# Moving seven pieces of side work, and splitting the mean term of a last layer norm into rows, in a two-block transformer kernel

## The chip, the cores and the metric

The kernel runs on one core of a Trainium2 chip. The metric is the device time of one execution in microseconds (us), the median of three runs. A profile is taken in an execution of its own, which has a time of its own.

## The reference

One sequence of 256 tokens and width 2048 goes through two blocks, all in fp32. The first block has four mixers side by side on one projection, an output projection, and a gated feed-forward. The second has an attention mixer and a retention mixer, each followed by a layer norm. Cut to the parts that the change touches:

```python
def first_block(x, ...):                       # T = 256, D = 2048
    h = rms_norm(x, norm_mix)
    a_q, a_kv, a_g, b_cols, c_cols, d_cols = jnp.split(h @ w_in, SPLIT_POINTS, axis=-1)
    o_a = nsa_attention(...)                   # heads with compressed, selected, window parts
    o_b = short_conv_mixer(b_cols, conv_w)     # 3-tap convolution times a gate
    o_c = spatial_gating_mixer(c_cols, sgu_w, sgu_b)   # gelu, layer norm, token mixing, gating
    o_d = stick_breaking_attention(dq, dk, dv)
    mixed = rms_norm(stack([o_a, o_b, o_c, o_d]), group_gain)
    x = x + mixed @ w_out
    h = rms_norm(x, norm_ffn)
    return x + (silu(h @ w_ffn_gate) * (h @ w_ffn_up)) @ w_ffn_down

def second_block(x, ...):
    y = attention_mixer(x, ...)                # q, k, v, gate; 16 heads; (o * silu(g)) @ w_out
    x = layer_norm(ALPHA * x + y, ln_gain[0], ln_bias[0])
    y = retention_mixer(x, ...)                # 8 heads forward and backward, group norm, gate
    return layer_norm(ALPHA * x + y, ln_gain[1], ln_bias[1])
```

## The kernel before

**Matrix products.** The weights come from HBM as units of up to 1024 columns by 128 rows (`wf`, fetched from SyncE's queue, four buffers). ScalarE rounds a unit into `wh` (L375) and VectorE forms the rest `wl = wf - wh` (L385), four buffers each. `job_T` multiplies a unit's 128x128 chunks with an activation tile that holds a high and a low part side by side: one matmul of 512 columns with `wh` (L452) and one of 256 with `wl` (L453), called a pair here. Four output tiles of 128 rows collect in four PSUM banks (`st`); at the end of a job an `evac` callback empties each bank. The last chunks of a job (`tail` of them) are run output by output, so that the four banks end one after the other instead of together. `job_N` is the same with the roles of weights and activations exchanged, three matmuls of 512 columns (L475 to L477). One matmul form with two extra columns (L441 to L443) serves the layer norm that is folded into the next projection.

**Side work.** Everything else (attention heads, gelus, norms, splitting of activations into high and low) is written as Python generators in a scheduler `S`. Each pair advances a counter, and every second pair is a tick; `yield n` puts the rest of a generator n ticks later. A generator only fixes where instructions are issued: each engine then runs its own in that order. When a matmul needs an activation tile that its generator has not made yet, `XS.__getitem__` forces the generator's remaining steps on the spot, in one burst. `S.drain` does the same.

**Stage a** is the projection `w_in` (jobs for the mixers A, D, C, B in turn) with the generators `task_A`, `task_D`, `task_C` and `by_task`/`task_B`; it ends with the job whose banks `ev_bb(2)` empties. `task_A` and `task_D` and `task_C` share two PSUM banks `mA`. `task_C` handles two halves of 128 tokens one after the other: gelu of `cv` (L702 to L710), a layer norm with `rsqrt` (a chain of ten tiny VectorE operations, L496 to L501), `v` scaled at L1043, gelu of `cu`, then the token mixing on PE (L1048), L1049 and L1051 on VectorE, and `finish_nat`: a square sum on ScalarE (L717), an `rsqrt`, transposes (L725) and the split into `xB` tiles (ScalarE L732, VectorE L738). **Stage b** is `w_out`: four jobs `wo(0)` to `wo(3)` that read the 16 tiles `xB` (0 to 3 from A, 4 to 7 from D, 8 to 11 from C, 12 to 15 from B) and whose banks VectorE empties (L1144, L1145). Inside `wo(0)` the tile `xB[8]` is wanted at pair 32 of 64, and a burst is forced there if `task_C` is not done.

**Bank emptying in `ev_bb`** (two output tiles, i = i0 and i0 + 1): ScalarE copies the right half (L662), VectorE adds the left (L664), then a product with `zy[i]` from `by_task(i)` (L1095), its square (L1100) and the sum `bacc` (L1101) run on GpSimd, and for the last tile (i = 3) on VectorE. `by_task` uses GpSimd at L1068, L1069 and L1077.

**Later.** The attention mixer of the second block makes its heads one after the other; `og_task` gates a head's output (L1522) and, ten ticks later, splits it (ScalarE L509, VectorE L511) for the output projection. In that projection, `stat(k)` adds each finished tile (L1432, L1434) to the sums of the next layer norm: a square on ScalarE (L1369), the sum on GpSimd (L1370), the sum of squares on GpSimd for k < 12 and on VectorE above (L1372). The column sums on PE (L1393) follow.

**The end.** The last layer norm needs mean and variance of full rows. After the last matmul, VectorE finishes the statistics and makes `nm = -mean * rstd` (L1990). For six of the eight 128x512 output pieces, the product of the gain with `nm` plus the bias is a K = 2 matmul in plain fp32 (L2004), from the rows `[nm, 1]` and `[gain, bias]`; L2011 adds it to the scaled row, and each piece is stored from the queue of SyncE or of ScalarE (L2012).

Of the kernel before, what the change touches and what calls it, by code (L numbers as in the profile page):

```python
# [9 lines left out]
F32 = mybir.dt.float32  # L10
F32R = mybir.dt.float32r
I32 = mybir.dt.int32
AF = mybir.ActivationFunctionType
OP = mybir.AluOpType
# [4 lines left out]
P = 128  # L19
T = 256  # L20
D = 2048
# [186 lines left out]
def pack_inputs(inp):  # L208

    f = {k: np.asarray(v) for k, v in inp.items()}  # L210
# [54 lines left out]
    qg, kg = f["attn_q_gain_2"][0], f["attn_k_gain_2"][0]  # L265
    out["v3"] = np.ascontiguousarray(rep(np.concatenate([qg, qg[sw], kg, kg[sw]])))
    c = shape_consts()
    out["lnv"] = np.ascontiguousarray(np.stack([f["ln_gain_2"][1], f["ln_bias_2"][1]]))
    out["ident"] = c["ident"]
    out["c1"] = np.concatenate([c[k] for k in C1], 1)  # L270
# [68 lines left out]
def body(tc, a, out, stop=None, dbg=None):  # L339
# [142 lines left out]
    def take():  # L482
        return jq.pop(0)
# [176 lines left out]
    def ev_sum(p, mk=s1):  # L660
        t = mk("evt")
        ACT.activation(t, p[:, T:], AF.Copy)  # L662
        s = mk("evs")
        V.tensor_tensor(s, p[:, :T], t, OP.add)  # L664
        return s
# [82 lines left out]
    def task_A():  # L748
# [36 lines left out]
        for tt in range(2):  # L785
# [25 lines left out]
                            gate[tt][:, 0:8].rearrange("p (g i) -> p i g", g=2), OP.mult)  # L811
            V.tensor_tensor(w, w, wt[:, :, None].to_broadcast([P, 8, nk]), OP.mult)
            V.tensor_tensor(w, w, cmk[:, None, 15 * tt:15 * tt + nk].to_broadcast([P, 8, nk]), OP.mult)
            yield 1
            pt = mA()
            PE.transpose(pt[:120, :P], sc, ident)
            pcT = small(128)
            V.tensor_copy(pcT[:120], pt[:120, :P])
            yield 1
            po = pm.tile([P, 512], F32, name="mO", tag="mO", bufs=1)  # L820
            PE.matmul(po, pcT[:120], vc[:120].rearrange("p c d -> p (c d)"), start=True, stop=True)
            per, nkt = (4, 1) if tt == 0 else (2, 2)
# [211 lines left out]
    def task_C():  # L1034
        yield tSg
        yield tD
        for tt in range(2):
            v = yield from gelu2(cv[tt], 512, s2)
            st_, mv, r = small(6), small(2), small()
            V.bn_stats(st_, v)  # L1040
            V.bn_aggr(mv, st_)
            rsqrt(r, mv[:, 1:2], 1.0, 4e-5, 1)
            V.tensor_scalar(v, v, mv[:, 0:1], r, OP.subtract, OP.mult)  # L1043
            u = yield from gelu2(cu[tt], 512, s2)
            yield 1
            pz = mA()
            for h in range(8):
                PE.matmul(pz[:, h * 64:h * 64 + 64], sg[h // 4][:, h % 4, :], v[:, h * 64:h * 64 + 64], start=True, stop=True)  # L1048
            V.tensor_tensor(v.rearrange("p (h e) -> p h e", h=8), pz.rearrange("p (h e) -> p h e", h=8),  # L1049
                            sgb[:, :, None].to_broadcast([P, 8, 64]), OP.add)  # L1050
            V.scalar_tensor_tensor(u, u, 0.5, v, OP.mult, OP.mult)  # L1051
            yield 3
            yield from finish_nat(u, 8, tt, mA)
# [33 lines left out]
    def ev_bb(i0):  # L1087
        def f(m, p):
            i = i0 + m
            s = ev_sum(p)  # L1090
            S.drain(tBy[i])
            last = i == 3
            r = braw[i // 2][:, i % 2, :]
            e = V if last else G
            e.tensor_tensor(r, s, zy[i], OP.mult)  # L1095
            if nb[0] == 0:
                e.tensor_tensor(bacc, r, r, OP.mult)
            else:
                q = s1("bq")
                e.tensor_tensor(q, r, r, OP.mult)  # L1100
                e.tensor_tensor(bacc, bacc, q, OP.add)  # L1101
            nb[0] += 1
        return f
# [37 lines left out]
    def ev_wo(mm):  # L1141
        def f(m, p):
            k = 4 * mm + m
            V.tensor_tensor(xr[k], p[:, :T], xr[k], OP.add)  # L1144
            V.tensor_tensor(xr[k], p[:, T:], xr[k], OP.add)  # L1145

            def gen():
                yield 1
                x = newx("A", k)
                yield from split(x, xr[k], g2[:, k:k + 1])  # L1150
                xA2.t[k] = x
                yield 3
                sq_acc(k)
            xA2.by[k] = S.add(gen())
        return f
# [12 lines left out]
        return  # L1168
    S.drain(tA, tD)
    xr = load_x(lambda z: None)  # L1170
    job_T(take(), xB, ev_wo(0))
    S.drain(tA, tB, tC, tD)
    p1.close()
    p2 = ExitStack()
# [121 lines left out]
    class LN:  # L1296
# [65 lines left out]
        def stat(self, k):  # L1362
            yield 2
            if k == 0:
                G.tensor_copy(self.s, xr[k])
                ACT.activation(self.q, xr[k], AF.Square)
            elif k < 14 or self.done:
                sq = self.base.tile([P, T], F32, name="lnt", tag="lnt", bufs=3)
                ACT.activation(sq, xr[k], AF.Square)  # L1369
                G.tensor_tensor(self.s, self.s, xr[k], OP.add)  # L1370
                yield 1
                (G if k < 12 else V).tensor_tensor(self.q, self.q, sq, OP.add)  # L1372
                if self.done:
                    pass
                elif k == 11:
                    self.head()
                elif k == 13:
                    yield 2
                    self.sums(self.s, self.q, False)
            else:  # L1380
                sq = self.pool.tile([P, T], F32, name="lnu", tag=f"lnu{k}")
                ACT.activation(sq, xr[k], AF.Square)
                yield 4
                self.sums(xr[k], sq, k == 15)
            if self.done:
                yield 1
                yield from self.done(k)
# [131 lines left out]
    def og_task(h, o):  # L1519

        s = sl.pop(h)
        V.scalar_tensor_tensor(s, o, 0.5, s, OP.mult, OP.mult)  # L1522
        x = newx("A", h)
        yield 10
        yield from split(x, s)
        og.t[h] = x

# [405 lines left out]
    v = a["lnv"]  # L1933
    G.dma_start(gb, bass.AP(tensor=v.tensor, offset=v.offset, ap=[[0, P], [1, D]]))
    G.dma_start(ob, bass.AP(tensor=v.tensor, offset=v.offset + D + 3 * 512, ap=[[0, P], [1, 512]]))
    gr = q5.tile([P, D], F32, name="gr")
    G.dma_start(gr[:2], a["lnv"])
    nm = [q5.tile([P, 2], F32, name="nm", tag=f"nm{tt}") for tt in range(2)]
    nT = [q5.tile([P, P], F32, name="nT", tag=f"nT{tt}") for tt in range(2)]
    for tt in range(2):  # L1940
        V.memset(nm[tt][:, 1:2], 1.0)
    y5 = [q5.tile([P, 4, 512], F32, name="y5", tag=f"y5{tt}") for tt in range(2)]
    bs = [q5.tile([P, 4, 6], F32, name="bs", tag=f"bs{tt}") for tt in range(2)]
    res, tRes = {}, {}
# [41 lines left out]
    for tt in range(2):  # L1986
        V.bn_aggr(mv[:, 2 * tt:2 * tt + 2], bs[tt].rearrange("p a b -> p (a b)"))
    rsqrt(r, mv[:, 1::2], 1.0, 1e-5, 2)
    for tt in range(2):
        V.scalar_tensor_tensor(nm[tt][:, 0:1], mv[:, 2 * tt:2 * tt + 1], -1.0, r[:, tt:tt + 1], OP.mult, OP.mult)  # L1990
    pt = pm.tile([P, 512], F32, name="rt", tag="rt", bufs=2)
    for tt in range(2):
        PE.transpose(pt[:2, tt * P:tt * P + P], nm[tt], ident)
    for tt in range(2):
        y = y5[tt][:, 3]
        ACT.activation(y, y, AF.Identity, scale=r[:, tt:tt + 1], bias=nm[tt][:, 0:1])
        if tt == 0:
            for z in range(2):
                ACT.activation(nT[z][:2, :], pt[:2, z * P:z * P + P], AF.Copy)
    order = [(m, tt) for m in (3, 0, 1, 2) for tt in range(2)]  # L2000
    add = {}
    for m, tt in order[2:]:
        add[(m, tt)] = p = st()
        PE.matmul(p, nT[tt][:2, :], gr[:2, 512 * m:512 * m + 512], start=True, stop=True)  # L2004
    for n, (m, tt) in enumerate(order):
        y = y5[tt][:, m]
        if m == 3:
# [28 lines left out]
```

## Time and profile before

| | |
|---|---|
| time, three runs | 2285.02, 2287.87, 2290.71 us; median 2287.87 |
| profiled execution | 2299.29 us, its span 2297.5 us |
| mean granted TensorE clock | 0.995 of full speed |
| busy share of the span | PE 99%, DVE 67%, ACT 49%, POOL 18% |
| PE busy | 2271.2 us of 2297.5 |

The span runs from the first instruction to the last and leaves 1.8 us of the profiled execution outside. In the rows, PE is TensorE, DVE VectorE, ACT ScalarE and POOL GpSimd; `x4` is a count; a bracket at a row's end is the engine's idle time before it and what ended it. L numbers are lines of the kernel before.

### The profile page before, as it was taken

Reading aid. Unit: us, or ns where it says so; the run is one execution under the profiler, and the core shown is the slowest. Engines: PE = TensorE matmul, PEld = TensorE weight load, DVE = VectorE, ACT = ScalarE, POOL = GpSimd, SP = SyncE. Lnnn points to the kernel's source line nnn. Section 1 sums busy time; section 2 is a strip of 40 time slices with the busy share of each in tenths; the row PEclk is TensorE's granted clock in tenths of the full one; section 3 lists DMA queues with packets and bytes.
Section 4 is the critical chain, followed back from the end, with each engine's and each line's share of the span. In section 5 each row is a group of like instructions: output and inputs, shape, how many; then the busy total and the mean of one; then the engine's idle time right before and its main releaser. Section 6 shows DMA issues by size and latency. Waiting matters only on the chain.

```text
span 2297.5 us, 32746 instructions
## 1 busy us (share of the span) xinstructions
PE 2271.2 (99%) x12423; PEld 1946.4 (85%) x12423; DVE 1534.2 (67%) x2368; ACT 1134.2 (49%) x1661; POOL 406.4 (18%) x384
## 2 busy tenths in 40 slices
PE   8999999999999999999999999999999999999998
PEld 7877888888888888888888888898888888888886
DVE  6666697755555565555558898888776676766554
ACT  5457545544443354444444556555444544445442
POOL 2224341111110011110002211742000000001120
PEclk9999999999999999999999999999999999999998
DMA  7643355565565555656565444555555555556553
GB/s 248 231 147 119 111 187 189 184 187 189 187 191 189 179 190 187 188 184 190 186 201 183 141 152 153 179 168 199 175 167 174 183 167 187 168 174 216 189 179 118
DMA packets 113757, 409.82 MB, mean 178 GB/s; under 512 B 12816, under 2 KB 13072, under 8 KB 113342
## 3 DMA queue, kind: packets, MB, share of 16 engines
q1 hardware_dynamic: 111456, 399.75, 54.1%
q0 software_dynamic: 1424, 6.86, 0.9%
q8 instruction: 97, 1.59, 0.3%
q10 hardware_dynamic: 720, 1.13, 0.1%
q14 instruction: 60, 0.49, 0.1%
HBM read 405.57 MB, written 4.21 MB: 178 GB/s over the span
## 4 chain that ended last, share of the span: by engine, by line
PE 87%; DVE 5%; ACT 1%; issue 1%; POOL 1%; POOLq 0%; DVEq 0%; ACTq 0%
PE st L452 39%; PE st L453 20%; PE st L475 7%; PE st L477 7%; PE st L476 7%; DVE wl L385 2%; PE mO L1889 1%; PE mA L855 1%; PE mS L1862 0%; PE st L443 0%; PE st L441 0%; PE st L442 0%; PE st L2004 0%; PE mO L836 0%; PE mT L1907 0%
## 5 line engine op out<-in xcount | busy, mean ns | idle before, releaser
L375 ACT ACTIVATE wh<-wf 128x1024 fp32r<-128x1024 f32 (+1 forms) x750 | 789.7, 1055 | 731.7 <-PE st L452 381.1
L385 DVE TENSOR_TENSOR wl<-wf,wh 128x1024 fp32r<-128x1024 f32 (+1 forms) x750 | 954.8, 1282 | 287.8 <-ACT wh L375 287.1
L452 PE MATMUL st<-xA,wh 128*128 128x512 f32 x2016 | 722.6, 402 | 8.1 <-DVE xA L515 6.8
L453 PE MATMUL st<-xA,wl 128*128 128x256 f32 x2016 | 567.8, 282 | 1.7 <-DVE wl L385 1.5
L452 PE MATMUL st<-xB,wh 128*128 128x512 f32 x1440 | 511.4, 399 | 2.4 <-DVE evs L664 1.8
L452 PEld LDWEIGHTS st<-xA,wh 128*128 128x128 f32 x2016 | 380.9, 189 | 100.9 <-DVE xA L515 6.7
L453 PE MATMUL st<-xB,wl 128*128 128x256 f32 x1440 | 404.3, 281 | 0.0
L453 PEld LDWEIGHTS st<-xA,wl 128*128 128x128 f32 x2016 | 382.6, 190 | 2.9 <-DVE wl L385 2.5
L452 PEld LDWEIGHTS st<-xB,wh 128*128 128x128 f32 x1440 | 271.3, 188 | 67.0 <-DVE evs L664 2.5
L453 PEld LDWEIGHTS st<-xB,wl 128*128 128x128 f32 x1440 | 272.4, 189 | 1.0
L452 PE MATMUL st<-act,wh 128*128 128x512 f32 x704 | 248.8, 399 | 0.0
L453 PE MATMUL st<-act,wl 128*128 128x256 f32 x704 | 197.9, 281 | 0.0
L475 PE MATMUL st<-wh,xB 128*128 128x512 f32 x448 | 175.5, 392 | 0.0
L476 PE MATMUL st<-wl,xB 128*128 128x512 f32 x448 | 174.7, 390 | 0.0
L477 PE MATMUL st<-wh,xB 128*128 128x512 f32 x448 | 174.6, 390 | 0.0
L452 PEld LDWEIGHTS st<-act,wh 128*128 128x128 f32 x704 | 132.4, 188 | 32.9
L664 DVE TENSOR_TENSOR evs<-st,evt 128x256 f32<-128x256 f32 x110 | 46.2, 423 | 145.6 <-ACT evt L662 145.4
L453 PEld LDWEIGHTS st<-act,wl 128*128 128x128 f32 x704 | 133.0, 189 | 0.0
L475 PE MATMUL st<-wh,xA 128*128 128x512 f32 (+2 forms) x320 | 122.6, 383 | 0.0
L476 PE MATMUL st<-wl,xA 128*128 128x512 f32 (+2 forms) x320 | 118.3, 370 | 0.9 <-DVE wl L385 0.9
L477 PE MATMUL st<-wh,xA 128*128 128x512 f32 (+2 forms) x320 | 118.4, 370 | 0.0
L1211 POOL TENSOR_TENSOR evs<-evs,R 128x256 f32<-128x256 f32 x44 | 32.4, 735 | 484.5 <-DVE evs L664 484.5
(447 smaller groups left out, 2611.7 us busy)
## 6 DMA issues: line engine op xcount, KB each, us to landing
wf<-in_w_c SPq DMA_DIRECT2D x264, 512.0 KB, 4.2
wf<-in_w_e SPq DMA_DIRECT2D x256, 512.0 KB, 3.8
wf<-in_w_d SPq DMA_DIRECT2D x112, 512.0 KB, 3.5
wf<-in_w_a SPq DMA_DIRECT2D x84, 512.0 KB, 3.6
wf<-in_w_b SPq DMA_DIRECT2D x32, 512.0 KB, 4.3
xr<-in_xT SPq DMA_DIRECT2D x16, 256.0 KB, 5.4
wf<-in_w_a SPq DMA_DIRECT2D x5, 420.0 KB, 3.8
dr<-d POOLq DMA_DIRECT2D x1, 2048.0 KB, 10.1
```

What stands on the lines that cost most here:

```text
L375: ACT.activation(wh[q][:, :n], wf[q][:, :n], AF.Copy)
L385: V.tensor_tensor(wl[q][:, :n], wf[q][:, :n], wh[q][:, :n].bitcast(F32), OP.subtract)
L452: PE.matmul(ps[m], hv[:, cs], x, start=kk == 0, stop=False)
L453: PE.matmul(ps[m][:, :T], lv[:, cs], x[:, :T], start=False, stop=kk == K - 1)
L475: PE.matmul(p, xh, h[:, o:o + n], start=kk == 0, stop=False)
L476: PE.matmul(p, xh, l[:, o:o + n], start=False, stop=False)
L477: PE.matmul(p, xl, h[:, o:o + n], start=False, stop=kk == K - 1)
L664: V.tensor_tensor(s, p[:, :T], t, OP.add)
L855: PE.matmul(pv[:, y, :], qT[i // 2][64 * g:64 * g + 64, i % 2, tt * P:tt * P + P], kT[64 * g:64 * g + 64, b, 0:W], start=True, stop=True)
L1211: G.tensor_tensor(s, s, R2, OP.mult)
L1889: PE.matmul(po, l[:, st_, o], r_[:, st_], start=i == 0, stop=i == 5)
```

## The change

Seven places are edited. (1) `task_A` waits three ticks instead of one before its transpose and two instead of one after it. (2) `task_C` waits five ticks instead of one before the token mixing. (3) For the job of `ev_bb(2)`, ScalarE copies the whole bank and GpSimd adds the halves. (4) `wo(0)` runs its last two chunks output by output. (5) The sum of squares of the layer norm after the attention mixer stays on GpSimd for k of 12 and more. (6) The heads 13, 14 and 15 are split one tick after gating instead of ten. (7) The mean term of the last norm is a K = 5 matmul of fp32r rows: `nm` as high, high and low part and two rows of ones, against gain and bias as high and low parts, which the new `gr_task` prepares during the last jobs.

```diff
+    out["pick"] = np.ascontiguousarray(np.stack([[1, 0, 1, 1, 0], [0, 1, 0, 0, 1]], 1).astype(np.float32))
...
@@ task_A
-            yield 1
+            yield 3
             pt = mA()
             PE.transpose(pt[:120, :P], sc, ident)
             pcT = small(128)
             V.tensor_copy(pcT[:120], pt[:120, :P])
-            yield 1
+            yield 2
             po = pm.tile([P, 512], F32, name="mO", tag="mO", bufs=1)
...
@@ task_C
             u = yield from gelu2(cu[tt], 512, s2)
-            yield 1
+            yield 5
             pz = mA()
...
@@ ev_bb
-            s = ev_sum(p)
+            if i0:
+                c = s2("evc")
+                ACT.activation(c, p, AF.Copy)
+                s = c[:, :T]
+                G.tensor_tensor(s, s, c[:, T:], OP.add)
+            else:
+                s = ev_sum(p)
...
-    job_T(take(), xB, ev_wo(0))
+    job_T(take(), xB, ev_wo(0), 2)
...
@@ stat
-                (G if k < 12 else V).tensor_tensor(self.q, self.q, sq, OP.add)
+                (G if k < 12 or self.done else V).tensor_tensor(self.q, self.q, sq, OP.add)
...
@@ og_task
-        yield 10
+        yield 10 if h < 13 else 1
...
-    gr = q5.tile([P, D], F32, name="gr")
-    G.dma_start(gr[:2], a["lnv"])
...
+    pick = q5.tile([P, 2], F32, name="pick")
+    G.dma_start(pick[:5], a["pick"])
+    gr = q5.tile([P, 3 * 512], F32R, name="gr")
+    def gr_task():
+        yield 8
+        for m in range(3):
+            t = q5.tile([P, 512], F32, name="res", tag="res", bufs=4)[:5]
+            h = q5.tile([P, 512], F32R, name="grh", tag="grh", bufs=1)[:5]
+            for z, (lo, hi) in enumerate(((0, 3), (3, 5))):
+                G.dma_start(t[lo:hi], bass.AP(tensor=v.tensor, offset=v.offset + z * D + 512 * m,
+                                              ap=[[0, hi - lo], [1, 512]]))
+            yield 12
+            o = gr[:5, 512 * m:512 * m + 512]
+            ACT.activation(h, t, AF.Copy)
+            V.tensor_tensor(t, t, h.bitcast(F32), OP.subtract)
+            V.tensor_scalar(t, t, pick[:5, 1:2], None, OP.mult)
+            V.scalar_tensor_tensor(o, h.bitcast(F32), pick[:5, 0:1], t, OP.mult, OP.add)
+            yield 4
+    S.add(gr_task())
...
-    for tt in range(2):
-        V.scalar_tensor_tensor(nm[tt][:, 0:1], mv[:, 2 * tt:2 * tt + 1], -1.0, r[:, tt:tt + 1], OP.mult, OP.mult)
+    V.scalar_tensor_tensor(nm, mv[:, 0::2], -1.0, r, OP.mult, OP.mult)
+    V.tensor_copy(nx[:, :, 0:2], nm[:, :, None].to_broadcast([P, 2, 2]))
+    V.tensor_tensor(nx[:, :, 2], nm, nx[:, :, 0].bitcast(F32), OP.subtract)
...
-        PE.matmul(p, nT[tt][:2, :], gr[:2, 512 * m:512 * m + 512], start=True, stop=True)
+        PE.matmul(p, nT[tt][:5, :], gr[:5, 512 * m:512 * m + 512], start=True, stop=True)
```

## Rows read from the trace of the kernel before

**Rows 1.** The page's first part: busy time of each engine, its share of the span and its instructions.

```profile
PE 2271.2 (99%) x12423; PEld 1946.4 (85%) x12423; DVE 1534.2 (67%) x2368; ACT 1134.2 (49%) x1661; POOL 406.4 (18%) x384
```

**Rows 2.** The waits of PE over the whole span, grouped: PE's tile and line, what it waited for; total us, times, longest us.

```profile
PE st L452 <- DVE evs L664: 1.8, 2, 1.1
...
PE mA L1048 <- DVE gq L1043: 1.3, 1, 1.3
PE st L452 <- DVE xA L511: 1.3, 2, 0.8
...
PE mA L816 <- DVE sm L813: 1.2, 2, 0.9
PE st L443 <- DVE wl L385: 1.2, 1, 1.2
...
PE st L452 <- DVE xr L1145: 0.6, 1, 0.6
...
PE mO L821 <- DVE sm L818: 0.4, 1, 0.4
```

**Rows 3.** Busy time in chosen stretches: from:to, length, then busy us of PE, PEld, DVE, ACT, POOL with counts; PEclk is the granted TensorE clock as a share of full speed; last the DMA share and GB/s.

```profile
296.70:300.10 3.40, 3.40 (x12) 2.87 (x11) 3.37 (x5) 2.67 (x4) 0.21 (x1) 0.50 0.79 205
...
330.82:334.24 3.42, 3.42 (x12) 2.89 (x11) 3.07 (x11) 1.06 (x1) 0.06 (x1) 0.50 0.07 14
...
1525.49:1528.90 3.41, 3.41 (x18) 3.41 (x17) 2.96 (x16) 0.59 (x2) 0.00 (x0) 0.50 0.91 311
...
2283.30:2297.50 14.20, 10.05 (x12) 3.27 (x10) 6.58 (x10) 0.48 (x1) 0.00 (x0) 0.50 0.39 148
```

**Rows 4.** Timeline of PE in `wo(0)`: start us, duration us, engine, line, operation. The first three lie at the half clock, the last two (pairs 32 and 33) at the full one.

```profile
331.07 0.63 PE L452 MATMUL st<-xB,wh 128*128 128x512 f32 x1
331.50 0.42 PE L453 MATMUL st<-xB,wl 128*128 128x256 f32 x1
331.72 0.63 PE L452 MATMUL st<-xB,wh 128*128 128x512 f32 x1
...
342.92 0.40 PE L452 MATMUL st<-xB,wh 128*128 128x512 f32 x1
...
343.27 0.39 PE L452 MATMUL st<-xB,wh 128*128 128x512 f32 x1
```

**Rows 5.** Busy time from the start of `wo(0)` (326.49 us) to its pair 32, columns as in the third group.

```profile
326.40:334.30 7.90, 6.06 (x25) 4.75 (x24) 7.34 (x19) 3.23 (x6) 3.36 (x4) 0.78 0.25 80
334.30:343.00 8.70, 8.70 (x54) 7.72 (x54) 7.77 (x25) 3.38 (x7) 0.00 (x0) 1.00 0.98 365
```

**Rows 6.** Timeline at the start of `wo(0)`, DVE and POOL rows of the bank emptying and of `task_C`, and the first DVE split of C's tiles.

```profile
325.52 1.65 POOL L1077 TENSOR_TENSOR evs<-evs,R 128x256 f32<-128x256 f32 x1 [0.88 <-DVE evs L1075]
...
326.50 1.22 DVE L710 SCALAR_TENSOR_TENSOR gq<-gq,cu 128x512 f32<-128x512 f32 x1
...
327.98 0.67 DVE L1049 TENSOR_TENSOR gq<-mA,vec 128x512 f32<-128x512 f32 x1
328.13 0.74 POOL L1095 TENSOR_TENSOR braw<-evs 128x256 f32<-128x256 f32 x1 [0.96 <-DVE evs L664]
...
328.69 0.74 DVE L1051 SCALAR_TENSOR_TENSOR gq<-gq 128x512 f32<-128x512 f32 x1
328.95 0.94 POOL L1100 TENSOR_TENSOR bq<-braw 128x256 f32<-128x256 f32 x1
329.35 0.41 DVE L664 TENSOR_TENSOR evs<-st,evt 128x256 f32<-128x256 f32 x1
...
329.86 0.43 DVE L1095 TENSOR_TENSOR braw<-evs 128x256 f32<-128x256 f32 x1
...
341.76 1.12 DVE L738 SCALAR_TENSOR_TENSOR xB<-mA,vec,xB 128x128 fp32r<-128x128 f32 x4
```

**Rows 7.** The four executions of L1077: durations in ns, minimum, median and maximum, first and last start, operands.

```profile
L1077 POOL TENSOR_TENSOR evs<-evs,R x4: 728/736/1653, 266.0 to 325.5; 128x256 f32<-128x256 f32 x4
```

**Rows 8.** Timeline of the layer norm after the attention mixer: the first of VectorE's sums of squares, the split before PE's wait and that wait, and the column sum of squares on PE.

```profile
1516.60 0.41 DVE L1372 TENSOR_TENSOR lnq<-lnq,lnt 128x256 f32<-128x256 f32 x1
...
1519.60 0.85 POOL L1370 TENSOR_TENSOR lns<-lns,xr 128x256 f32<-128x256 f32 x1 [0.61 <-DVE xr L1434]
...
1521.58 2.35 DVE L385 TENSOR_TENSOR wl<-wf,wh 128x1024 fp32r<-128x1024 f32 x2
...
1523.89 0.59 PE L1393 MATMUL pcs<-ones,lnq 128*128 128x1 f32 x4
```

**Rows 9.** Timeline of the last head: its gating and its split.

```profile
1442.82 0.41 DVE L1522 SCALAR_TENSOR_TENSOR sl<-mO,sl 128x256 f32<-128x256 f32 x1
...
1445.17 0.41 DVE L511 TENSOR_TENSOR xA<-sl,xA 128x256 fp32r<-128x256 f32 x1
```

**Rows 10.** Timeline of the end, after the last product.

```profile
2282.80 0.69 DVE L2008 TENSOR_TENSOR y<-y,gb 128x512 f32<-128x512 f32 x1 [0.81 <-ACT y L1996]
...
2282.98 10.37 PE L2004 MATMUL st<-gr,nT 2*128 2x512 f32 x12 [0.53 <-ACT nT L1999]
...
2285.46 0.74 DVE L2011 SCALAR_TENSOR_TENSOR y<-y,sm,st 128x512 f32<-128x512 f32 x1
...
2293.45 0.75 DVE L2011 SCALAR_TENSOR_TENSOR y<-y,sm,st 128x512 f32<-128x512 f32 x1 [0.96 <-PE st L2004]
```

**Rows 11.** The two loads in the kernel before into tiles named `gr`, from GpSimd's queue (one is the gain and bias of the end, the other an earlier table): time from issue to landing.

```profile
DMA to landing us min/median/max: 4.5/6.0/7.5
```

More of the change, by code (lines that the diff above doesn't have):

```diff
@@ L1935, in body @@
     G.dma_start(ob, bass.AP(tensor=v.tensor, offset=v.offset + D + 3 * 512, ap=[[0, P], [1, 512]]))
-    gr = q5.tile([P, D], F32, name="gr")
-    G.dma_start(gr[:2], a["lnv"])
-    nm = [q5.tile([P, 2], F32, name="nm", tag=f"nm{tt}") for tt in range(2)]
-    nT = [q5.tile([P, P], F32, name="nT", tag=f"nT{tt}") for tt in range(2)]
-    for tt in range(2):
-        V.memset(nm[tt][:, 1:2], 1.0)
+    pick = q5.tile([P, 2], F32, name="pick")
[17 more added lines that the diff above has]
+    S.add(gr_task())
+    nm = q5.tile([P, 2], F32, name="nm")
+    nx = q5.tile([P, 2, 5], F32R, name="nx")
+    nT = [q5.tile([P, P], F32R, name="nT", tag=f"nT{tt}") for tt in range(2)]
+    V.tensor_copy(nx[:, :, 3:5], ones[:, 0:4].rearrange("p (a b) -> p a b", a=2))
     y5 = [q5.tile([P, 4, 512], F32, name="y5", tag=f"y5{tt}") for tt in range(2)]
@@ L1988, in body @@
     rsqrt(r, mv[:, 1::2], 1.0, 1e-5, 2)
-    for tt in range(2):
-        V.scalar_tensor_tensor(nm[tt][:, 0:1], mv[:, 2 * tt:2 * tt + 1], -1.0, r[:, tt:tt + 1], OP.mult, OP.mult)
+    V.scalar_tensor_tensor(nm, mv[:, 0::2], -1.0, r, OP.mult, OP.mult)
+    V.tensor_copy(nx[:, :, 0:2], nm[:, :, None].to_broadcast([P, 2, 2]))
+    V.tensor_tensor(nx[:, :, 2], nm, nx[:, :, 0].bitcast(F32), OP.subtract)
     pt = pm.tile([P, 512], F32, name="rt", tag="rt", bufs=2)
     for tt in range(2):
-        PE.transpose(pt[:2, tt * P:tt * P + P], nm[tt], ident)
+        PE.transpose(pt[:5, tt * P:tt * P + P], nx[:, tt].bitcast(F32), ident)
     for tt in range(2):
         y = y5[tt][:, 3]
-        ACT.activation(y, y, AF.Identity, scale=r[:, tt:tt + 1], bias=nm[tt][:, 0:1])
+        ACT.activation(y, y, AF.Identity, scale=r[:, tt:tt + 1], bias=nm[:, tt:tt + 1])
         if tt == 0:
             for z in range(2):
-                ACT.activation(nT[z][:2, :], pt[:2, z * P:z * P + P], AF.Copy)
+                ACT.activation(nT[z][:5, :], pt[:5, z * P:z * P + P], AF.Copy)
     order = [(m, tt) for m in (3, 0, 1, 2) for tt in range(2)]
```

## The prediction

> **What bounds the kernel now.** I read the busy shares first: PE is busy 2271.2 us of a span of 2297.5 [rows 1]. Nothing here removes matrix products except at the very end, so the change can only win in the 26.3 us in which PE idles, in the stretches where PE runs at a lower clock, and in the tail behind the last product. The list of PE's waits says what the idle time is [rows 2]: seven of its entries are aimed at by edits 1 to 6, 1.2 + 0.4 us (`task_A`), 1.3 (`task_C`), 1.8 (banks at `wo(0)`), 0.6 (banks at `wo(1)`), 1.2 (split late in the layer norm) and 1.3 (last heads), 7.8 us in all. The windows by clock come next [rows 3]: three stretches of 3.4 us have a granted clock of 0.5, the 1.2 GHz level, and each begins 0.5 to 3 us after PE resumed from one or two of these waits; so does the tail, from 2283.3 to the end. A pair takes 0.35 us at the full clock, 2.4 GHz, and 0.65 at the lower [rows 4], so 3.42 us hold 5.3 pairs that would have taken 1.86: each such stretch costs 1.6 us. A wait itself costs its length and some 0.15 us for refilling the pipe (an estimate: the starts on either side of the waits lie that much further apart). Last I read VectorE around `wo(0)`: 15.1 us busy of 16.6 [rows 5], which makes it nearly a second bound there.
>
> **The change, part by part** (negative is time saved).
>
> *End, edit 7: -4.3.* L2004 shows 12 instructions for six plain fp32 matmuls, 10.37 us at the half clock [rows 10], 1.73 each. As fp32r a 512-column product is one instruction, 0.43 from start to start at this clock [rows 4], 2.6 in all. VectorE's work then bounds the end: the four operations L2008 and L2009 start at 2282.80, the first L2011 at 2285.46, and the last starts at 2293.45 because each waits for PE [rows 10]. With no wait the six follow each other at their own 0.74, so the last starts at 2285.46 + 5 x 0.74 = 2289.16, that is 4.3 earlier. The new `nx` costs two tiny VectorE operations ahead of the transposes, but the copies of the transposes on ScalarE are behind a 0.8 us activation anyway. Stores: 148 GB/s at a DMA share of 0.39 [rows 3] is 380 GB/s when busy, 0.69 us for 256 KB, so a store each 0.74 keeps up, narrowly. Bounds: -3.0 (the last two stores queue up) and -4.7. The preparation `gr_task` is hidden behind the last jobs, three times one ScalarE and three VectorE operations on five partitions; its cover is the 12 ticks (8.5 us at 0.71 a tick) between issuing the loads and reading them, and the nearest loads from this queue landed after 4.5 and 7.5 us [rows 11].
>
> *Last heads, edit 6: -1.0.* L1522 of the last head ends at 1443.23 and its L511 only at 1445.58 [rows 9], behind a weight split. Issued nine ticks earlier, the split of head 15 comes as soon as L1522 allows. Of 1.3 us and two refills (1.6) I take 1.0, since head 15 still needs two operations after L1522; bounds -0.3 and -1.6.
>
> *Layer norm, edit 5: -1.2.* Four VectorE operations of 0.41 or more (1.7 to 2.2 us with gaps) leave the queue ahead of the split L385 at 1521.58, for which PE waits 1.2 [rows 2, 8]. They go to GpSimd, where the like sum takes 0.85, beside the one already there: 1.6 per tile against a tile every 1.4 us, so GpSimd is late by under 1 us at the last tile, and the column sum that reads it starts at 1523.89 [rows 8]. I take 0.75 of the wait and about a third of the half-clock stretch at 1525.49 [rows 3]; bounds 0 and -3.0. GpSimd's L1077 takes 0.73 at best and 1.65 at worst [rows 7], the worst beside VectorE's L710 [rows 6]. The Trainium skill ("SBUF — State Buffer", section "SBUF: two separate sides") says that GpSimd and a VectorE operation with two operands from this memory share a port pair which the first takes for its whole instruction while the other is blocked. The row agrees in direction; by this rule the four sums would still hold VectorE up, edit 5 would be worth nothing, and the whole sum would be 1.2 poorer.
>
> *`task_A`, edit 1:* by itself -1.6 for the two entries, less new waits, because its later steps meet `task_D` in the two shared banks; the nearest row of such a clash in `task_C` or `task_A` is 1.3 at the most. I take -0.4, bounds -1.8 and +1.
>
> *`task_C`, `ev_bb` and `wo(0)`, edits 2 to 4.* What they remove: 1.3 + 0.15 at L1048 with the half-clock stretch at 296.7 (1.6), 1.8 + 0.3 at the banks with the stretch at 330.8 (1.6), and 0.7 at `wo(1)`; 7.4 in all. If that were everything, PE would reach pair 32 of `wo(0)` at 342.92 - 7.2 = 335.7 (the 6.8 ahead of it, and edit 1). But pair 32 reads `xB[8]` from `task_C`, and its first VectorE split starts at 341.76 [rows 6], hardly ahead of the pair's 342.92. It was issued, counted from the yields, at tick 15, one before the pair. Now both halves of the task wait four ticks more: the token mixing of the second half falls to tick 7 of `wo(0)` and its split to tick 23, so a burst is forced at pair 32. What sets its time is VectorE's queue. In the job's last output (i = 3), VectorE's L1095 now waits for GpSimd, where five operations stand ahead: the sum of i = 2, L1095, L1100, L1101 and the sum of i = 3, 0.74 to 0.94 each [rows 6], 4.1 us after L1077 has ended at 327.17, so 331.2, or about 330.2 if L1077 comes a microsecond earlier with PE. VectorE is free for it from 327.72 [rows 6] and has nothing else to run ahead of it: L1049 and L1051 (1.41) filled this time before and are now behind it. So L1095 starts 0.35 later, 1.41 is added after it, 0.44 of idle time further on can be filled (estimate from the 1.5 us idle [rows 5]): the split starts at 341.76 + 0.35 + 1.41 - 0.44 = 343.1, `xB[8]` is there at 343.4, and PE, early by 7, waits. Pair 32 comes at 343.4 against 342.92: +0.5 in place of -7.2, edits 1 and 2 included. Such a wait, longer than any that preceded a half-clock stretch, brings one of 1.6. Edit 4 keeps its -0.7. Together +1.4; bounds -7.8 (nothing late) and +4 (the forced transposes and copies, four of ScalarE among them, each wait for the one before).
>
> Sum: -4.3 - 1.0 - 1.2 + 1.4 = -5.1. Against the profiled 2299.29 us, that is 2294.2. The median shown is 11.4 lower than the profiled execution; I take the saving over unchanged, 2287.87 - 5.1 = 2282.8.
>
> **The rivals.** *All seven work as meant*: VectorE's queue catches up, or the burst finds its operands there, and the gains at `wo(0)` hold: -4.3 - 1.0 - 1.2 - 7.8 = -14.3, 2273.6; with the third half-clock stretch gone entirely, 2272.5. For it speaks that the waits are real and that each edit removes the cause of one; against it, 15.1 busy of 16.6 us on VectorE. *The tail gain is swallowed*: the stores queue behind each other and the end moves by 1.5 instead of 4.3, everything else as summed: 2285.6, no change. Against it: the busy rate of the stores above. *Slower*: ScalarE's copy in `gr_task` waits for its loads. It stands in front of the weight roundings L375; each load that lands later than the 8.5 us of cover by x holds up ScalarE by x, and past some 2 us of prefetched weights, PE too. Loads that land after 7.5 us [rows 11] leave 1 us. To turn -5.1 into more than +6.9, three copies would have to cost PE 4 us each, landing after 14 us: about 2295 if 15. GpSimd's queue, from which they are issued, carries sums ahead of them, which speaks for some delay, not for so much. *The change doesn't do its work*: the banks and the heads were late for another reason (ScalarE's rather than VectorE's), and only the tail is won: 2287.87 - 4.3 + 1.4 = 2285.0.
>
> **How the numbers follow.** About 0.3% (6.9 us) is what a measurement of this kernel can tell from no change. My forecast, VectorE holding pair 32 so that only the later edits count, has 0.48, with a range of its own of 2279 to 2287; all as meant 0.32; swallowed tail or no effect 0.12; slower 0.08. Faster by over 6.9 (below 2281.0) are the second case and a third of the first, 0.48; slower 0.08; within 0.44. The range reaches into the second case: 2274.0 to 2289.0 leaves out about 0.1 below and 0.08 above.
>
> **What would show it.** In the profile after: L2004 as six instructions of about 0.43 and L2011 without waits, the last row of L2011 some 6 us after the first row of L2008; no wait of PE for L511, and a shorter one for L385 near 1522; no waits for L664 at pairs 2 and 3, but one of several microseconds near pair 32 for L738 (or for what feeds it), with VectorE idle in front of L1095 for the GpSimd sum, and a half-clock stretch behind it. The prediction is wrong if VectorE reaches L1095 without waiting, if pair 32 starts within a microsecond after pair 31, or if PE waits in the last jobs for a weight rounding behind `gr_task`.

## The result and the profile after

The changed kernel takes 2304.48 us, the median of its runs, against 2286.44 for the kernel before on the same chip: 1.0072 times as long, with a 95% interval of 1.0051 to 1.0093. One of its four runs took 5202.78 us and stands in that median; the other three took 2301.76 to 2305.17. It is slower by 18 us where 5 us less were forecast, and lies outside the range. The profiled executions hide most of it (span 2300.0 against 2297.5), because the feed-forward jobs of any of these kernels run at one of two steady paces for a whole execution, and the profiled one of the kernel before had the slower, worth 13.8 us between 420 and 1190 us (last section); so the two traces are set side by side only up to 420 us and behind 1190 us.

Counted by the weight splits (the 750 instructions of L385, numbered from 0), this is how many us later the n-th starts in the changed kernel than in the kernel before, and in the kernels of the experiments that matter most:

```
split number (start before)   changed  edit 1 only  edits 2-7  edits 2-4  edit 2 only  edit 3 only  edits 4-7
 45 (148.6)                     -0.1      -0.7        0.0       -0.9       -0.2         +0.1       -0.5
 60 (214.5)                     +9.6      +8.1        0.0       -0.8       -0.3         +0.1       -0.4
 75 (285.0)                    +14.4     +12.9        0.0       -0.8       -0.3         +0.1       -0.4
 90 (336.4)                    +15.5     +13.2       +0.8       -0.1       -0.2         +1.5       -0.4
105 (382.6)                    +20.4     +13.8       +6.8       +6.7       +5.9         +3.6       -0.8
```

Two stretches lose: 14.5 us between 150 and 285 us, where `task_A` and `task_D` run, and 6 between 285 and 383, around `wo(0)`. What the second half wins, 4 us, comes almost all in the tail: between these two traces split 420 starts 6.6 us late and the last one 6.7.

The waits of PE in the changed kernel over the whole span, as in [rows 2] (lines behind L266 are one to some thirty higher than before; L845 and L872 are L844 and L871):

```profile
PE mA L845 <- POOL pr L872: 8.4, 8, 3.4
...
PE st L454 <- DVE wl L386: 3.0, 2, 1.5
PE pb L549 <- DVE bdg L546: 2.7, 1, 2.7
PE st L453 <- ACT evc L1093: 2.6, 1, 2.6
PE mA L726 <- DVE jk L721: 2.0, 1, 2.0
...
PE st L453 <- DVE xB L739: 1.7, 1, 1.7
PE mA L856 <- ACT pT L847: 1.4, 2, 0.7
...
PE lpb L1420 <- ACT lndg L1423: 1.1, 1, 1.1
PE st L453 <- DVE xA L512: 0.8, 1, 0.8
...
PE st L444 <- DVE wl L386: 0.4, 1, 0.4
```

Each of the waits that were aimed at is gone or smaller: L813, L1043, L664, L1145 are not in the list. In their place stand longer ones behind the same engines. `task_A`'s transposes wait eight times for GpSimd's product, the banks of `wo(0)` wait for ScalarE's copy, and L454, L549, L726 and pair 32 (`xB`, L739) wait for VectorE.

The windows at the half clock, with columns as in [rows 3]:

```profile
177.75:181.16 3.41, 3.41 (x9) 2.65 (x8) 3.01 (x4) 3.38 (x7) 0.43 (x1) 0.50 0.25 73
205.05:211.88 6.83, 5.55 (x14) 3.90 (x15) 2.26 (x4) 2.51 (x3) 2.51 (x2) 0.50 0.26 78
273.32:276.73 3.41, 3.41 (x11) 2.58 (x10) 2.76 (x5) 0.00 (x0) 0.00 (x0) 0.50 0.02 5
341.58:345.00 3.42, 3.09 (x9) 2.67 (x10) 0.54 (x1) 1.22 (x2) 3.18 (x5) 0.50 0.47 153
358.65:365.48 6.83, 5.09 (x17) 4.13 (x16) 5.21 (x12) 3.38 (x8) 0.00 (x0) 0.50 0.72 229
```

There are 24 us at 1.2 GHz before the tail, against 10.2 [rows 3]. Between 120 and 285 us the kernel before had 2.9 us of waits and none of these windows; the changed one has 11.8 us of waits and 13.6 us at the half clock, which cost about 6 (46% of it, by the pairs of 0.65 and 0.35 us [rows 4]). The 8.9 us of added waits and these 6 make 15, against the 14.5 of the table.

### The profile page after: what moved, and what is told of

Its sections match the earlier page's. It is cut to its first block, busy times and chain, and to the rows that moved or that the text cites. A ratio compares the mean times of both kernels' runs of the same rounds, so it can differ in the third digit from the quotient of the medians.

```text
span 2300.0 us, 32765 instructions
## 1 busy us (share of the span) xinstructions
PE 2256.7 (98%) x12417; PEld 1946.8 (85%) x12417; DVE 1540.8 (67%) x2371; ACT 1137.3 (49%) x1664; POOL 416.4 (18%) x396
## 4 chain that ended last, share of the span: by engine, by line
PE 86%; DVE 4%; ACT 1%; issue 1%; POOL 1%; DMA 0%; SPq 0%; DVEq 0%; POOLq 0%; ACTq 0%
PE st L453 39%; PE st L454 20%; PE st L476 7%; PE st L477 7%; PE st L478 7%; DVE wl L386 1%; PE mO L1896 1%; PE mS L1869 0%; PE mA L856 0%; PE st L442 0%; PE st L444 0%; PE st L443 0%; POOL pr L872 0%; PE mT L1914 0%; ACT wh L376 0%
## 5 line engine op out<-in xcount | busy, mean ns | idle before, releaser
L453 PE MATMUL st<-xA,wh 128*128 128x512 f32 x2016 | 713.8, 397 | 7.6 <-DVE xA L516 6.7
L454 PE MATMUL st<-xA,wl 128*128 128x256 f32 x2016 | 566.4, 281 | 3.0 <-DVE wl L386 3.0
L454 PE MATMUL st<-xB,wl 128*128 128x256 f32 x1440 | 404.9, 281 | 0.0
L454 PEld LDWEIGHTS st<-xA,wl 128*128 128x128 f32 x2016 | 382.8, 190 | 4.1 <-DVE wl L386 3.8
L454 PEld LDWEIGHTS st<-xB,wl 128*128 128x128 f32 x1440 | 273.5, 190 | 1.1
L453 PE MATMUL st<-act,wh 128*128 128x512 f32 x704 | 244.1, 391 | 0.0
L454 PE MATMUL st<-act,wl 128*128 128x256 f32 x704 | 197.1, 280 | 0.0
L454 PEld LDWEIGHTS st<-act,wl 128*128 128x128 f32 x704 | 133.1, 189 | 0.0
```

Of the source, the lines that this page charges most:

```text
L453: PE.matmul(ps[m], hv[:, cs], x, start=kk == 0, stop=False)
L454: PE.matmul(ps[m][:, :T], lv[:, cs], x[:, :T], start=False, stop=kk == K - 1)
```

## The experiments

Ratios are to the kernel before on the same chip, with their 95% intervals; before stood at 2285.9 to 2286.4 us in these comparisons. Where an execution has the slower of the two paces of the last section, its time lies some 8 us or more above the rest of its kernel's, as the traced executions show; up to 3 in 10 have it. Medians and ratios mix both paces; "at the faster pace" marks a difference of means without that upper group, with its 95% interval.

**Edit 1 alone.**

```diff
-            yield 1
+            yield 3
             pt = mA()
             PE.transpose(pt[:120, :P], sc, ident)
...
-            yield 1
+            yield 2
             po = pm.tile([P, 512], F32, name="mO", tag="mO", bufs=1)
```

> The kernel before with edit 1 alone (task_A waits 3 and 2 ticks). Theory A (the shifted steps of task_A fall behind steps of task_D in the in-order queues of ScalarE, VectorE and GpSimd; PE then waits at the transposes behind the GpSimd product): slower by about 14 us, 2300, with PE waits of 8 us or more for that product and two to four stretches at the half clock between 150 and 300 us. Rival (the loss in this stage comes from edits 1 and 2 together, task_C's wait included): within 3 us of the kernel before.

Measured: 2303.11 us, 1.0071 (1.0056 to 1.0086). Theory A's size is about right (17.2 by the medians, 13.8 by the trace at split 105), and the rival falls. The waits of PE between 120 and 285 us are those of the changed kernel, to a tenth: besides the group shown, 2.0 for L720 and 1.4 for L846.

```profile
PE mA L844 <- POOL pr L871: 8.4, 8, 3.4
```

**Edits 2 to 7, without edit 1** (the change with `task_A` put back).

> Edits 2 to 7, without edit 1. Theory A: the 14 us of the stretch from 150 to 300 us are gone; left are the loss at the first output job (about +5), the end (-4) and the heads (-1): 2286, within 3 us of the kernel before. Rival (edit 1 is not the cause): 2300.

Measured: 2289.69 us, 1.0025 (1.0003 to 1.0046), 3.8 over the kernel before (3.1 at the faster pace, +-1.3), just outside theory A's 3. The stretch from 150 to 285 us is that of the kernel before (0.0 in the table). Edit 1 is the larger cause, and the rest still loses a little, at `wo(0)`. By the trace the two parts add up: 13.8 and 6.8 against 20.4 at split 105.

**Edit 7 alone** (the end).

> The kernel before with edit 7 alone (the mean term from split rows). As in the sum of the prediction: -4.3 us, 2282. Rival (the stores queue up, or the preparation holds up ScalarE in the last jobs): -1 to +3. Its profile also shows a second time how long the feed-forward jobs between 420 and 1190 us take in a kernel that has no edit there.

Measured: 2282.79 us, 0.9984 (0.9974 to 0.9994), 3.1 less by the medians (3.3 at the faster pace, +-0.9). Its trace shows the same six fp32r instructions as the changed kernel, and no wait of PE in the last jobs. The rival falls; the gain is three quarters of what was forecast by the times.

**Edits 2, 3 and 4 together.**

> The kernel before with edits 2, 3 and 4 (gating, bank emptying, tail of the first output job). Theory B (these lose by themselves: VectorE waits at its product for GpSimd's sums, and the tiles of task_C are forced late): slower by 2 to 7 us, 2288 to 2293, with PE waits at the square-sum product, at xB[8] and for ScalarE's copy. Rival (they only lose because task_A and task_D end late in the changed kernel): faster by 3 to 7, 2280 to 2283.

Measured: 2293.6 us, 1.0033 (1.002 to 1.0046); the medians stand 7.7 apart (8.3 at the faster pace, +-1.1). Its split 105 starts 6.7 us late with nothing wrong before 285 us, so the loss at `wo(0)` is its own. The waits of PE from 285 to 365 us:

```profile
PE pb L548 <- DVE bdg L545: 2.7, 1, 2.7
PE st L452 <- ACT evc L1092: 2.6, 1, 2.6
PE st L452 <- DVE xB L738: 2.5, 1, 2.5
PE st L453 <- DVE wl L385: 1.5, 1, 1.5
```

They make 9.3 us, against 3.7 in the same stretch before. Its timeline shows the two mechanisms at the banks:

```profile
325.15 0.63 ACT L708 ACTIVATE gq<-gq 128x512 f32<-128x512 f32 x1 [3.25 <-POOL gq L706]
...
325.69 0.58 ACT L1092 ACTIVATE evc<-st 128x512 f32<-128x512 f32 x1
...
330.86 0.42 DVE L1101 TENSOR_TENSOR braw<-evc,evs 128x256 f32<-128x256 f32 x1 [4.33 <-POOL evc L1094]
```

ScalarE stands 3.25 us in front of the tanh L708 for GpSimd's L706, and the copy that frees the bank is queued behind it: 2.6 us of PE. VectorE stands 4.33 us in front of its product for the fifth GpSimd operation in a row.

**Edit 2 alone** (`task_C` waits 5 ticks instead of 1).

> The kernel before with edit 2 alone (task_C waits 5 ticks). If the forced burst at xB[8] is the larger half of the loss at the first output job: the 1.3 us wait at the token mixing goes, another of 1.5 for a weight split comes in its place as in the run with edits 2 to 4, and a wait of 2 or more appears before pair 32; slower by 2 to 5 us. If the burst only costs because VectorE's queue is late there (edit 3): within 2 us, either way.

Measured: 2291.98 us, 1.0035 (1.0013 to 1.0057), 5.9 more (6.3 at the faster pace, +-0.9). PE waits from 285 to 365 us:

```profile
PE st L452 <- DVE evs L664: 3.5, 1, 3.5
PE st L452 <- DVE xB L738: 2.3, 1, 2.3
PE st L453 <- DVE wl L385: 1.5, 1, 1.5
...
```

The wait of 1.3 for L1043 is gone and 1.5 for the weight split L385 stand in its place, at 295.6 us: the split lies behind the same chain of VectorE operations. PE is then early at the banks and waits 3.5 there instead of 1.8, 1.2 for L545 (not shown), and 2.3 in front of pair 32. No edit of the banks is needed for this loss.

**Edit 3 alone** (ScalarE copies, GpSimd adds).

> The kernel before with edit 3 alone (ScalarE copies, GpSimd adds). Theory B: VectorE idles 3 to 4 us in front of its product for i = 3, the square-sum product and the tiles of task_C come late, and the banks come free later rather than earlier because ScalarE's copy stands behind the tanh of task_C: slower by 3 to 7 us. Rival (edit 3 frees the banks as meant and only together with edit 2 loses): faster by 1 to 4.

Measured: 2288.11 us, 1.0007 (0.9984 to 1.003). The ratio hides the loss, because 6 of the 31 executions of the kernel before and 1 of these 10 had the slower pace: at the faster pace it is 2.6 more (+-0.9), and by the trace split 105 starts 3.6 late. So theory B's mechanism is there (VectorE idles 2.84 us in front of L1101), at or just under the lower end of its price of 3 to 7 us, and the rival falls: edit 3 loses without edit 2. PE's waits from 285 to 365 us:

```profile
PE mA L725 <- DVE jk L720: 2.8, 2, 2.1
PE st L453 <- DVE sm L496: 2.1, 1, 2.1
...
PE st L452 <- ACT evc L1092: 0.4, 1, 0.4
```

With those left out they make 7.2 us, against 3.7 before. The banks come free as meant, 0.4 us of waiting instead of 1.8; the gain is taken back, and more, at the next two products of VectorE, the split in front of `rsqrt` and L720.

**Edits 4 to 7, without 1 to 3.**

> Edits 4 to 7 without 1 to 3. By the terms of the prediction: -0.7 - 1.2 - 1.0 - 4.3 = -7.2 us, 2279. By the trace of the changed kernel, in which the layer norm gained nothing net (a wait of 1.1 for its last scale came in place of 1.2 for the split): about -5.5, 2280.5.

Measured: 2281.07 us, 0.9975 (0.996 to 0.999), 5.0 less (4.5 at the faster pace, +-0.8). It is the fastest of all kernels here.

**The first wait of edit 1 alone** (`yield 3` before the transpose, the second `yield` as before).

> The kernel before with the first half of edit 1 alone (3 ticks ahead of task_A's transpose; a shift of 2 ticks per half instead of 3). Theory A takes the phase between task_A and task_D as the cause, so a different shift gives a different loss, not two thirds of it: anything from 0 to +15. Rival (each added tick costs the same): +10.

Measured: 2287.68 us, 0.9995 (0.9966 to 1.0024): by the times alone hardly told from no change (2.1 more at the faster pace, +-1.1). By the trace split 75 is 1.0 late and split 105 0.4. Two thirds of the delay cost an eighth of the loss or less.

**The second wait of edit 1 alone** (`yield 2` after the transpose).

> The kernel before with the second half of edit 1 alone (2 ticks instead of 1 between task_A's transpose and its product; task_A is 1 tick later from its first half on, 2 from its second). Theory A (what counts is where task_A's later steps fall against task_D's, and shifts of 2 and 4 ticks cost 1.6 us, 3 and 6 cost 17): within 4 us of the kernel before. Rival (this second wait itself is the dear one): +10 or more.

Measured: 2291.49 us, 1.0033 (1.0011 to 1.0055), 5.1 more (4.8 at the faster pace, +-1.3), between the two expectations. A shift of 1 and 2 ticks costs more than one of 2 and 4, and the two waits alone make 2 and 5 us where both together make 17: the price is neither one per tick nor that of one of the two places.

**Edit 1 in the first half of `task_A` only.**

```diff
-            yield 1
+            yield 1 if tt else 3
...
-            yield 1
+            yield 1 if tt else 2
```

> The kernel before with both waits of edit 1 in the first half of task_A alone, so that it is 3 ticks later from 125 us on and stays 3 later in its second half. Theory A: the wait of 2.0 us at 176 and others like it stay, as in the run with edit 1 up to 184 us; slower by 4 to 15. Rival (the second half's waits make the loss): within 2 us.

Measured: 2291.25 us, 1.0016 (1.0002 to 1.0031), 4.9 more (5.4 at the faster pace, +-1.0). The wait at 176 us stands as in the changed kernel, and the timeline shows what makes it:

```profile
171.26 0.88 DVE L499 TENSOR_TENSOR sm<-sm 128x1 f32<-128x1 f32 x1
...
172.08 2.55 POOL L1028 TENSOR_TENSOR sg<-sg,c 128x512 f32<-128x512 f32 x2
172.17 1.22 DVE L500 SCALAR_TENSOR_TENSOR sm<-sm 128x1 f32<-128x1 f32 x1
173.42 1.22 DVE L501 SCALAR_TENSOR_TENSOR sm<-sm 128x1 f32<-128x1 f32 x1
...
176.72 0.66 PE L725 MATMUL mA<-ident,jk 128*128 128x128 f32 x4 [2.05 <-DVE jk L720]
```

Three operations of `rsqrt` on one element per partition, 0.16 us each elsewhere, take 0.88, 1.22 and 1.22 while GpSimd ends L960 of `task_D` (until 172.12) and runs two products L1028 of 1.3 us: 2.8 us more in a chain that PE then waits 2.05 for. Three ticks earlier, in the kernel before, the chain was over at 169.24, and GpSimd's products began at 169.15.

**The same with `task_D` started three ticks later too** (`yield 3` as the first step of `task_D`).

> As the run before it, with task_D started 3 ticks later as well, so that task_A and task_D stand to each other as in the kernel before. Theory A: the waits at the transposes between 150 and 280 us fall back to those of the kernel before (1.2 us in all, 3 waits) and no stretch at the half clock lies there; task_C, which waits for task_D, comes 3 ticks later and may cost up to 4 us at the first output job as the gating run did. Rival (task_A's lateness by itself costs, against the jobs on PE and not against task_D): the loss of the run before stays.

Measured: 2291.65 us, 1.0015 (0.9994 to 1.0035). In the stretch, half of the loss goes: split 60 is 1.9 us late instead of 4.1, split 75 1.7 instead of 3.5. The wait at 176 us and its window at the half clock are gone: `rsqrt` ran at 0.16 and was over at 171.32, ahead of GpSimd's products from 172.07 on. Other waits of 1.1, 0.9 and 0.8 stay, and a window at 188 us. So the phase to `task_D` counts, but is not all: theory A had expected 1.2 us of waits and no such window. By the medians the run as a whole gained nothing, with times that scatter from 2286 to 2302; by the traces split 120 is 4.4 late instead of 5.7, so a part of the gain is lost again around `wo(0)`.

**Edits 4 to 7 with edit 3 mended**: for i = 3, VectorE adds the halves itself.

```diff
-            s = ev_sum(p)
+            if i0:
+                c = s2("evc")
+                ACT.activation(c, p, AF.Copy)
+                s = c[:, :T]
+                (V if m else G).tensor_tensor(s, s, c[:, T:], OP.add)
+            else:
+                s = ev_sum(p)
```

> Edits 4 to 7 and edit 3 mended: for the last output (i = 3) VectorE adds the halves itself from ScalarE's copy, so its product waits for no GpSimd sum. Theory B (VectorE's wait for GpSimd is what made edit 3 lose): the banks come free by ScalarE's copy, VectorE has no idle time of 4 us, and 1 to 4 us are won over the run with edits 4 to 7: 2277 to 2280. Rival (the copy of the whole bank behind the tanh is what costs): 2281 or more.

Measured: 2284.48 us, 0.9989 (0.9965 to 1.0013), 3.4 over the run with edits 4 to 7 by the medians; by the splits 2.1 of it arises between 285 and 383 us. VectorE no longer stands still, and yet:

```profile
330.02 0.97 DVE L1095 TENSOR_TENSOR evc<-evc 128x256 f32<-128x256 f32 x1
...
331.77 0.84 DVE L1107 TENSOR_TENSOR bq<-braw 128x256 f32<-128x256 f32 x1
...
336.86 1.11 PE L726 MATMUL mA<-ident,jk 128*128 128x128 f32 x4 [2.14 <-DVE jk L721]
```

The three operations that replaced the wait run beside GpSimd's at 0.97, 0.65 and 0.84 us instead of 0.42, and PE waits at the same L726 as long as with edit 3 unmended (2.14 and 2.13 us). Theory B falls as to the cause: VectorE's stop in front of one product is not needed for the loss. The rival's mechanism is not seen either, since PE waits only 0.4 us for ScalarE's copy. That it is VectorE's queue as a whole is argued, not shown.

**`task_D` after `task_A`, without and with edit 1** (`yield tA` as the first step of `task_D`).

> The kernel before with task_D started only when task_A is done. The whole run is much longer (task_D and task_C are then forced in a burst ahead of the first output job); only the stretch from 120 to 285 us counts, where task_A now runs against the jobs alone. It is the base of the next run: the waits for task_A's operands in this stretch as in the kernel before or less, 1 to 3 us in all.

> As the run before it, with edit 1. Theory A (edit 1 loses because task_A's later steps fall behind task_D's in the engines' queues): without task_D beside it edit 1 does what it is for, and the stretch from 120 to 285 us is up to 2 us shorter than in the run before it, with no stretch at the half clock. Rival (task_A's steps, later by 3 and 6 ticks, clash with the jobs' own emptying and splitting): 8 us or more longer, with the long waits at the transposes.

Measured: 2337.91 and 2355.32 us in single runs, which only the stretch from 120 to 285 us is read from. The waits of PE from 120 to 300 us, first without and then with edit 1:

```profile
PE mA L816 <- DVE sm L813: 1.1, 2, 0.8
PE mA L844 <- POOL pr L871: 0.6, 1, 0.6
```

```profile
PE mA L844 <- POOL pr L871: 3.9, 6, 1.1
```

With `task_D` away, edit 1 adds 2.2 us of waits and one window at the half clock, and the splits 80 and 85 start 2.4 and 3.9 us later than they would (those up to the 35th ran 0.9 ahead). Beside `task_D` it added 8.9 us of waits and, in the run with edit 1 alone, three windows. Both expectations are missed, theory A's of up to 2 us less and the rival's of 8 more. By these two traces, one of each kernel, theory A carries some 11 of the 14.5 us (an estimate); the other 3 to 4 come without `task_D`, and edit 1 does not win anything even alone.

## Why the prediction was wrong, point by point

**Edit 1, the step that failed worst: -0.4, bounds -1.8 and +1; measured +17 by the medians, +13.8 by the trace at split 105.** The prediction removed two entries of 1.6 us and bounded the loss by the longest single wait of such a clash in the trace. But the yields stand ahead of sixteen later passes of `task_A`'s loop, six in the first half and ten in the second, and twelve of them run a chain through VectorE, ScalarE, VectorE, GpSimd and PE in whose queues `task_D` has its own chain. The dearest, in the changed kernel, reads:

```profile
201.10 0.49 ACT L868 ACTIVATE pr<-pr,sm 128x256 f32<-128x256 f32 x1
...
202.08 0.58 ACT L949 ACTIVATE az<-mB 128x512 f32<-128x512 f32 x1
...
202.69 0.69 DVE L951 TENSOR_SCALAR zm<-mB 128x512 f32<-128x512 f32 x1 [4.64 <-ACT az L949]
...
203.90 0.15 DVE L870 RECIPROCAL sm<-sm 128x2 f32<-128x2 f32 x1
204.08 0.16 DVE L871 TENSOR_TENSOR sm<-sm,gate 128x2 f32<-128x2 f32 x1
204.48 1.80 POOL L872 TENSOR_TENSOR pr<-pr,sm 128x512 f32<-128x512 f32 x1 [3.42 <-ACT wh L376]
206.33 1.12 PE L845 MATMUL mA<-ident,pr 128*128 128x128 f32 x4 [3.42 <-POOL pr L872]
```

`task_A`'s exponentials L868 are done at 202.2, but VectorE cannot take its tiny L870 before L951 of `task_D`, which waits for L949, which ScalarE had behind those exponentials; L870 comes 1.7 us late, GpSimd's product after it, and PE stands 3.42 us, with 6.83 us at the half clock around it. The two banks `mA` are not in this chain. The clash over them that the prediction reckoned with is a small part of what happened: 1.4 of the 11.8 us, where L856 waits for the copy L847 that empties a bank. The half clock, 13.6 us of it here, was not in this term at all, though the text had its price of 1.6 a stretch.

**Edits 2 to 4: +1.4 with edit 1's part; measured +7.7 without it. The path to pair 32 failed.** The prediction was right that PE's gains ahead of `xB[8]` would come back as waits and that VectorE would stand in front of its product for GpSimd (4.33 us, forecast about 2.5; the product started at 330.86, forecast 330.2). The step that failed is "What sets its time is VectorE's queue": the first split L738 was forecast at 343.1 and started at 347.23, after VectorE had stood idle for 2.35 us. In the run with edits 2 to 4:

```profile
342.76 0.89 PE L548 MATMUL pb<-bdg,ones 128*128 128x256 f32 x2 [2.67 <-DVE bdg L545]
...
345.12 1.06 ACT L375 ACTIVATE wh<-wf 128x1024 fp32r<-128x1024 f32 x1 [1.03 <-DMA wf<-in_w_b]
...
347.23 1.12 DVE L738 SCALAR_TENSOR_TENSOR xB<-mA,vec,xB 128x128 fp32r<-128x128 f32 x4 [2.35 <-ACT xB L732]
...
347.64 0.80 PE L452 MATMUL st<-xB,wh 128*128 128x512 f32 x1 [2.49 <-DVE xB L738]
```

PE stands for the norm of mixer B (L545) and runs L548, and `task_C`'s transposes L725 come only behind it, at 344.10; ScalarE then rounds a weight unit, for which it waits 1.03 us, ahead of the copies L732 at 346.08. Pair 32 starts at 347.64, 4.2 after the forecast 343.4. The prediction had this path, but only as its upper bound of +4. Nor was PE early by 7: waits of 1.5 for a split, 2.6 for the bank that ScalarE's copy frees and 2.7 for L545 had taken the gains, and pair 31 started at 343.10, against 342.38 before. PE stood 13.6 us at the half clock in that stretch instead of the forecast 3.4.

**Edit 7: mechanism right.** Forecast -4.3; -3.1 by the medians, and by the trace of the changed kernel -4.2: from the first L2008 to the end of the span 14.7 us before (2282.80 to 2297.5) and 10.5 after (2289.50 to 2300.0).

```profile
2289.50 0.69 DVE L2036 TENSOR_TENSOR y<-y,gb 128x512 f32<-128x512 f32 x1 [0.48 <-ACT y L2024]
...
2289.90 2.36 PE L2032 MATMUL st<-gr,nT 5*128 5x512 f32 x6 [0.36 <-ACT nT L2027]
...
2292.16 4.03 DVE L2039 SCALAR_TENSOR_TENSOR y<-y,sm,st 128x512 f32<-128x512 f32 x6
```

Six products take 2.36 us (forecast 2.6) and the six operations 4.03 without a wait (forecast 4.4); the stores nearly keep up: the span ends 3.8 us behind the last operation, against 3.3 before. The rival in which ScalarE waits for `gr_task`'s loads cost nothing: PE has no wait in the last jobs.

**Edits 5 and 6: too high.** Forecast -1.2 for the layer norm, -1.0 for the heads; neither was run alone. From split 420 to split 650, which takes in both, the four traces with these edits run between 0.5 us faster and 0.2 slower than the kernel before, and nine others (all but the two that hold `task_D` back) 0.5 to 2.7 slower. So nothing to some 1 us was won, of 2.2. Of the head waits 0.8 of 1.3 us stay, those of the last head, and the same 0.8 is left in the nine traces without edit 6. The wait for the split falls from 1.2 to 0.4, but 1.1 for L1423 appears behind it, where runs without edit 5 have 0.6 or none. The half-clock stretch at 1525 is gone, but it is also missing in three traces without edit 5 (edit 1, edit 7 and the first wait, each alone). The rival by which edit 5 is worth nothing shows in the changed kernel:

```profile
1527.31 2.88 DVE L386 TENSOR_TENSOR wl<-wf,wh 128x1024 fp32r<-128x1024 f32 x2
1527.40 1.72 POOL L1379 TENSOR_TENSOR lnq<-lnq,lnt 128x256 f32<-128x256 f32 x1
```

The last sum on GpSimd takes 1.72 us instead of 0.74 beside the two splits, and these take 2.88 instead of 2.35. The 1.65 of L1077 in [rows 7] fits the same pair better than L710: the split L385 ran from 325.36 to 326.58 in the kernel before, and L710 behind it took 1.22 us, against 0.69 in the run with edits 2 to 4. Edits 4 to 7 together were forecast at -7.2 and measured at -5.0.

**The chances.** Slower had 0.08, by a mechanism (`gr_task`) that held up nothing. The two mechanisms that did were both in the text, as terms with tight bounds: edit 1's was the length of one wait, and of the half clock only one stretch, at pair 32, was counted. The signs named for `wo(0)` all came true in the changed kernel (VectorE idle in front of its product, waits near pair 32, a half-clock stretch there), and none of the signs of being wrong did: the largest loss, edit 1's, had no sign of its own.

## What to carry to other kernels

A `yield` ahead of a long generator moves all its later steps against every other generator in the same queues. The longest wait seen so far is no bound for that: 1.3 us was taken here, and PE then waited eleven times, up to 3.4 us, and stood 13.6 us at the lower clock. Where a second engine is busy nine tenths of a stretch, a wait of PE removed there can come back at that engine's next product: edits 2 and 3, ahead of `xB[8]`, each lost when run alone, and edit 7, the one that won alone, lies behind the last product. And before two traces or two medians are compared, see which pace each execution had.

## What the hardware showed that was not expected

VectorE's tiny operations with two inputs stretch from 0.16 to 1.22 us, the length of the GpSimd products beside them, while the two with one input ahead of them did not (0.14 and 0.15 us at 170.90 and 171.07 in the run with edit 1's first half). The Trainium skill ("SBUF — State Buffer", section "SBUF: two separate sides") says so for a VectorE operation with two operands from this memory against a GpSimd one that reads it: the first takes the shared pair for its whole instruction. The trace agrees. A larger operation pays about as much: L957 of 128x512, 0.69 us elsewhere, took 1.78 at 172.10 beside a GpSimd product in the run with `task_D` shifted. So a chain of tiny ones, which can pay it at each, loses most for its work.

The feed-forward jobs, where no engine is waited for, ran at 0.347 us a pair on average in the changed kernel's profile and 0.353 in that of the kernel before, with the same instructions and a granted clock of 1.00. The rows, first of the changed kernel, then of the kernel before, are five pairs apart:

```profile
619.94 0.39 PE L453 MATMUL st<-xA,wh 128*128 128x512 f32 x1
...
621.67 0.39 PE L453 MATMUL st<-xA,wh 128*128 128x512 f32 x1
```

```profile
619.67 0.40 PE L452 MATMUL st<-xA,wh 128*128 128x512 f32 x1
...
621.44 0.40 PE L452 MATMUL st<-xA,wh 128*128 128x512 f32 x1
```

Between splits 120 and 400 that is 13.8 us, and of the profiles taken here some had the one pace and some the other (edit 7 alone the slower, edit 1 alone the faster). The kernel before had the slower one in its profile and, by its times, the faster one in most runs, so most of the 11.4 us that the prediction found between the two is this. What sets the pace of an execution was not found.
